# A sparse-attention layer on one core: the first stage's order of work, its input loads and its table stores are rewritten

## The chip, the cores and the metric

The kernel runs on one NeuronCore of one Trainium2 chip. The metric is device microseconds (us) of one execution. Five engines run at once, each through its own list of instructions in order: PE (TensorE: matmuls and transposes; its weight loads are listed as PEld), DVE (VectorE), ACT (ScalarE), POOL (GpSimd) and SP (SyncE, which here issues the DMAs). A tile scheduler orders each engine's list when the kernel is built and adds the semaphore waits.

## What is computed

One layer of native sparse attention with a gated branch, in float32, for 512 positions of width 1024, 16 heads of 64 in 4 groups:

```python
y = rms_norm(x, pre_gain)
q, kv, g, z = split_cols(y @ w_in, [1024, 6 * 256, 48, 3 * 1024])
k_c, v_c, k_s, v_s, k_w, v_w = split(kv, 6)
kc, vc = compress_kv(k_c, ...), compress_kv(v_c, ...)   # 31 blocks of 32 positions, + pos, then a 2-layer MLP
o_cmp, p_cmp = nsa_compressed(q, kc, vc, table)         # softmax(q kc + bias) vc
o_slc = nsa_selected(q, k_s, v_s, select_blocks(p_cmp), table)
o_win = nsa_window(q, k_w, v_w, table)
out = x + rms_norm((sum over 3 branches of gate * o * silu(z)) @ w_out, post_gain)
```

The bias of all three softmaxes comes from one table of 32 distance buckets by 16 heads.

## The kernel before

Every float32 product is made of three passes of a rounded type: each operand is split into a high part (a cast) and a low part (the operand less its high part), and PE adds high x high, low x high and high x low into one PSUM bank (`pass3`, L246). So each 512 KB weight tile `wr` (128x1024 numbers, 3 buffers) needs a cast into `wh` (L113 on ACT or L115 on DVE) and two subtractions into `wl` (L118, on POOL or DVE, 3 buffers each). Loads stand on SP's queue; a `wr` buffer is loaded again when its split is done, and `wh`, `wl` are written again when their matmuls are done. `tile_(n)` (L242) splits two tiles ahead; `order` (L226) lists the weights: 0, 1 for the compressed keys' projection `kc`, 2, 3 for `vc`, then four pairs (rows of the values' weights, rows of the keys' MLP weights `mk`), then pairs of key, query and gate weights with the values' MLP weights `mv`. Odd tiles are split on DVE alone, even ones on ACT and POOL (L240).

**The first stage** (L260 to L379) loads `x` in four tiles `xt` of 128 positions. `rms(t)` (L304) sums squares of a tile on ACT, and `rstd` (L84) makes the factor `r` on POOL in two steps. `prep(t)` (L311) does for each half of 512 columns: scale on DVE (L316), four transposes on PE into one bank (L321), two casts into `uh` (L327, ACT) and two subtractions into `ul` (L328, DVE). `uh`, `ul` are the normalized input, transposed, which every projection reads. `kc` is then made in two halves of 256 positions (`hh`, L368): per row block `k` and bank `m` the three passes in turn (L247 to L249, 96 matmuls of 256 columns). `prep(2)`, `prep(3)` stand inside the first half. `tables()` (L330) makes the bias table rows `toep` (4 matmuls, L344, L345) and the compressed branch's bias `cb` (16 matmuls of 16 columns, L351, L352), stores both to DRAM (L347, L356) and calls `load_bias(0)` (L160), which reads them back in shifted layouts.

**The second stage** (L381 on) makes `vc` (`half_t(2)`, `half_t(3)`: 48 matmuls of 512 columns into two `s` banks, L454), turns both projections into overlapping blocks (`blocks`: eight additions L407 from PSUM on DVE, then four casts and four subtractions L417 on DVE and POOL), and then runs the pairs: 24 matmuls of a value tile into four banks (`pj`, `pj`, `s`, `o`; L480 to L482) and 12 of an `mlp` (L425 to L427). After it come the keys, the queries, the gates, and from about 113 us the attention units, which the change doesn't touch.

Of the kernel before, what the change touches and what calls it, by code (L numbers as in the profile page):

```python
# [51 lines left out]
def nsa_layer(ctx: ExitStack, tc: tile.TileContext, x, pre_gain, post_gain, table, w_in, w_out,  # L52
# [39 lines left out]
    uh = [keep.tile([128, 2, S], F32R, name=f"uh{i}", tag="u", bufs=8) for i in range(4)]  # L92
    ul = [keep.tile([128, 2, S], F32R, name=f"ul{i}", tag="u", bufs=8) for i in range(4)]
# [152 lines left out]
    def pass3(po, wh_, wl_, rh, rl, first, last):  # L246
        T.matmul(po, wh_, rh, start=first, stop=False)  # L247
        T.matmul(po, wl_, rh, start=False, stop=False)  # L248
        T.matmul(po, wh_, rl, start=False, stop=last)  # L249

    def half_t(n, kh, banks):
        h, l = tile_(n)
        for kk in range(4):
            k = kh * 4 + kk
            for m, p in enumerate(banks):
                ms = slice(m * 128, m * 128 + 128)
                pass3(p, h[:, kk, ms], l[:, kk, ms], uh[k // 2][:, k % 2, :], ul[k // 2][:, k % 2, :],
                      k == 0, k == KT - 1)

    with tc.tile_pool(name="a1", bufs=1) as a1:  # L260
# [7 lines left out]
        V.tensor_copy(ones, one)  # L268
        xs = []
# [29 lines left out]
        banks = [tb, ob, tb]  # L299
        nb_ = 0  # L300

        rs_ = {}

        def rms(t):  # L304
            ss = a1.tile([128, 1], F32, name="ss", bufs=4)
            tc.keep_in_program_order(A.activation(sq, xs[t], AF.Square, scale=1.0 / 32, accum_out=ss))
            r = a1.tile([128, 1], F32, name="r", bufs=4)
            rstd(r, ss)
            rs_[t] = r

        def prep(t):  # L311
            nonlocal nb_
            r = rs_[t]
            for kq in range(2):
                hs = slice(kq * 512, (kq + 1) * 512)
                V.scalar_tensor_tensor(xs[t][:, hs], xs[t][:, hs], r, gain[kq], op0=ALU.mult, op1=ALU.mult)  # L316
                p = banks[nb_ % 3]()
                nb_ += 1
                for j in range(4):
                    k = kq * 4 + j  # L320
                    T.transpose(p[:, j * 128:(j + 1) * 128], xs[t][:, k * 128:(k + 1) * 128], ident)  # L321
                for jj in range(2):
                    i = kq * 2 + jj
                    src = p[:, jj * 256:(jj + 1) * 256].rearrange("p (a b) -> p a b", a=2)
                    dh = uh[i][:, :, t * 128:(t + 1) * 128]
                    dl = ul[i][:, :, t * 128:(t + 1) * 128]
                    A.copy(dh, src)  # L327
                    V.tensor_tensor(dl, src, dh.bitcast(F32), op=ALU.subtract)  # L328

        def tables():  # L330
            ntab = a1.tile([33, H], F32, name="ntab")
            V.tensor_scalar(ntab[0:32], tabx[0:32], -1.0, None, op0=ALU.mult)
            V.memset(ntab[32:33], BIG)
            nth = a1.tile([33, H], F32R, name="nth")
            ntl = a1.tile([33, H], F32R, name="ntl")
            V.tensor_copy(nth, ntab)
            V.tensor_tensor(ntl, ntab, nth.bitcast(F32), op=ALU.subtract)
            hsr = a1.tile([33, LT], F32R, name="hsr")
            hcr = a1.tile([33, D], F32R, name="hcr")
            A.copy(hsr, hots)  # L340
            A.copy(hcr, hotc)
# [19 lines left out]
        prep(0)  # L361
        split_ahead(0)
        prep(1)
        split_ahead(1)
        rms(2)
        rms(3)
        p_kc = [pj(), pj()]
        for hh in range(2):  # L368
            hs = slice(hh * 256, (hh + 1) * 256)
            for k in range(KT):  # L370
                if hh == 0 and k in (3, 5):
                    prep(2 if k == 3 else 3)
                h, l = tiles[k // 4]
                for m in range(2):
                    ms = slice(m * 128, m * 128 + 128)
                    pass3(p_kc[m][:, hs], h[:, k % 4, ms], l[:, k % 4, ms], uh[k // 2][:, k % 2, hs],
                          ul[k // 2][:, k % 2, hs], k == 0, k == KT - 1)
            if hh == 0:
                tables()  # L379

    with tc.tile_pool(name="a2", bufs=1) as a2:  # L381
        nb = G * NCMP

        def load_pos(nm):
            pr = small[nm, "p"]
            V.tensor_copy(pr[:, 1], pr[:, 0])
            p = tb()
            T.transpose(p[:, :32], pr.rearrange("p a b -> p (a b)"), ident[:32, :32])
            pt = sm.tile([128, 32], F32, name="pt" + nm)
            V.tensor_copy(pt, p[:, :32])  # L390
            return pt
# [10 lines left out]
        def blocks(banks, pt):  # L402
            blk = keep.tile([128, 16, G, NCMP], F32, name="blk", tag="kd", bufs=4)
            for m, p in enumerate(banks):
                for gp in range(2):
                    for lp in range(2):
                        V.tensor_tensor(  # L407
                            blk[lp * 64:lp * 64 + 64, :, 2 * m + gp, :],
                            view(p[gp * 64:gp * 64 + 64, :], lp, [[2, 16], [16, NCMP]]),
                            view(pt[gp * 64:gp * 64 + 64, :], lp, [[2, 16], [0, NCMP]]), op=ALU.add)  # L410
# [38 lines left out]

        kpt = load_pos("k")  # L450
        vpt = load_pos("v")
        kb = blocks(p_kc, kpt)
# [4 lines left out]
        kw2h, kw2l = load_w2("k", 2)  # L457
        vw2h, vw2l = load_w2("v", 1)
# [13 lines left out]
        for kp in range(4):  # L472
            h, l = tile_(n)
            for kk in range(2):
                k = kp * 2 + kk
                a, b = (v.rearrange("p (k a) c -> p k (a c)", k=2)[:, kk] for v in (h, l))
                for t in range(NT):
                    ts = slice(t * 128, (t + 1) * 128)
                    sh, sl = uh[k // 2][:, k % 2, ts], ul[k // 2][:, k % 2, ts]
# [4 lines left out]
            n += 2  # L484
        hs = silu2(p_mk)
# [307 lines left out]
    def split_y(g, qt):  # L793
        if g not in yhl:
# [3 lines left out]
            else:  # L798
                yhl[g] = [keep.tile([128, 2, S], F32R, name=f"y3{i}", tag="u", bufs=8) for i in range(2)]
# [20 lines left out]
    def wout():  # L820
        turn = [0, 3, 2, 1]
        og = [keep.tile([128, D], F32, name="og", tag="u", bufs=8) for _ in range(NT)]
# [38 lines left out]
        w3 = [wo_tile(3, 0, [keep.tile([128, 4, 256], F32R, name="w3", tag="u", bufs=8) for _ in range(2)]),  # L861
# [165 lines left out]
```

## Time and profile before

| | before |
|---|---|
| three timed runs | 466.29, 466.47, 467.47 us (median 466.47) |
| the profiled execution | 466.85 us, of which the span is 465.0 us |
| busy in the span | PE 450.9 us, PEld 375.3, DVE 330.6, ACT 274.3, POOL 184.7 |
| DMA | 44.63 MB, mean 96 GB/s |
| mean granted TensorE clock | 0.993 of full speed |

An engine's busy time says what it was doing, not what set the end. PE is busy nearly all the time, and its matmuls overlap (the end of each is modelled), so its pace is read from the distance between the starts of neighbours. Where PE loses time, a row shows either a gap and its releaser, or a longer distance between starts. The stretch from 0 to 45 us holds the work that the change rewrites.

### The profile page before, as it was taken

The page shows a single profiled execution, that of the slowest core. Times are in us where ns is not written, and L with a number is a line of the kernel's source. Part 1 is how long each engine was busy: PE and PEld are TensorE (multiplying, and loading weights), DVE is VectorE, ACT ScalarE, POOL GpSimd, SP SyncE. Part 2 cuts the span into 40 slices and gives each one's busy share as a digit, 9 for nine tenths or more (in the row PEclk, how much of TensorE's full clock was granted, in tenths as well). Part 3 has the DMA queues.
Part 4 walks back from the last instruction along what each step waited for, and adds up shares of the span by engine and source line. Part 5 has one row for each costly group of instructions (what it writes and reads, how often), then busy time and mean ns, then how long its engine had stood idle before and what let it go on. Part 6 is the DMA issues. An engine that isn't in the chain of part 4 may idle for free.

```text
span 465.0 us, 6924 instructions
## 1 busy us (share of the span) xinstructions
PE 450.9 (97%) x2330; PEld 375.3 (81%) x2330; DVE 330.6 (71%) x801; ACT 274.3 (59%) x642; POOL 184.7 (40%) x185
## 2 busy tenths in 40 slices
PE   5999999999999999999999999999999999999994
PEld 4797888878888878888888788888878888888883
DVE  6869844851766888768769776885896667567685
ACT  5712232542766577767846867666776666467541
POOL 4424544242223453342463525245343342448212
PEclk9989999999999999999999999999999999999998
DMA  8489275263111321511132332024051211214113
GB/s 300 142 82 280 77 216 162 66 206 90 47 45 48 112 59 34 182 45 47 45 90 70 88 94 71 21 57 132 19 180 45 92 45 47 91 43 140 47 45 135
DMA packets 45501, 44.63 MB, mean 96 GB/s; under 512 B 7751, under 2 KB 38471, under 8 KB 45466
## 3 DMA queue, kind: packets, MB, share of 16 engines
q1 hardware_dynamic: 44424, 44.00, 31.9%
q8 instruction: 18, 0.29, 0.3%
q10 hardware_dynamic: 1042, 0.20, 0.2%
q14 instruction: 17, 0.14, 0.1%
HBM read 41.99 MB, written 2.20 MB: 95 GB/s over the span
## 4 chain that ended last, share of the span: by engine, by line
PE 89%; DVE 4%; ACT 3%; issue 2%; POOL 1%; DVEq 0%; POOLq 0%; ACTq 0%
PE ps_pj L146 11%; PE ps_pj L148 11%; PE ps_pj L147 11%; PE ps_s L591 9%; PE ps_t L681 7%; PE ps_o L715 4%; PE ps_o L714 4%; PE ps_pj L834 3%; PE ps_pj L835 3%; PE ps_pj L836 3%; PE ps_s L247 2%; PE ps_s L248 2%; PE ps_s L249 2%; PE ps_pj L247 2%; PE ps_pj L248 1%
## 5 line engine op out<-in xcount | busy, mean ns | idle before, releaser
L118 POOL TENSOR_TENSOR wl<-wr,wh 128x512 fp32r<-128x512 f32 x94 | 123.0, 1328 | 138.6 <-ACT wh L113 122.2
L146 PE MATMUL ps_pj<-uh,wh 128*128 128x512 f32 x240 | 99.0, 412 | 0.0
L148 PE MATMUL ps_pj<-ul,wh 128*128 128x512 f32 x240 | 94.2, 393 | 0.0
L147 PE MATMUL ps_pj<-uh,wl 128*128 128x512 f32 x240 | 94.2, 392 | 0.0
L604 ACT ACTIVATE p<-p,nm 128x512 f32<-128x512 f32 (+3 forms) x128 | 71.6, 560 | 24.3 <-DVE nm L603 23.5
L685 DVE TENSOR_TENSOR ptl<-ps_t,pth 128x512 fp32r<-128x512 f32 x80 | 55.0, 688 | 28.2 <-ACT pth L684 27.7
L113 ACT CAST wh<-wr 128x1024 fp32r<-128x1024 f32 x47 | 49.2, 1047 | 43.5 <-DMA wr<-in_nsa_w_in_dram 20.1
L591 PE MATMUL ps_s<-kd,q 128*128 128x512 f32 (+5 forms) x256 | 63.9, 336 | 0.7 <-DVE zs L699 0.6
L684 ACT CAST pth<-ps_t 128x512 fp32r<-128x512 f32 x80 | 46.4, 580 | 29.3 <-PE ps_t L681 28.7
L148 PEld LDWEIGHTS ps_pj<-ul,wh 128*128 128x128 f32 x240 | 45.1, 188 | 10.1
L591 PEld LDWEIGHTS ps_s<-kd,q 128*128 128x128 f32 x256 | 43.9, 189 | 9.0 <-DVE zs L699 1.2
L146 PEld LDWEIGHTS ps_pj<-uh,wh 128*128 128x128 f32 x240 | 45.2, 188 | 6.1
L147 PEld LDWEIGHTS ps_pj<-uh,wl 128*128 128x128 f32 x240 | 45.3, 189 | 5.8
L603 DVE CUSTOM_DVE_ANT_0 p<-ps_s,bias 128x128 f32<-128x128 f32 (+3 forms) x80 | 34.6, 447 | 20.7 <-PE ps_s L591 20.5
L681 PE MATMUL ps_t<-ident,p 128*128 128x128 f32 x320 | 48.4, 272 | 0.0
L681 PEld LDWEIGHTS ps_t<-ident,p 128*128 128x128 f32 x320 | 39.7, 140 | 9.4
L714 PE MATMUL ps_o<-pth,vt 128*128 128x512 f32 x80 | 33.7, 421 | 0.0
L603 DVE CUSTOM_DVE_ANT_1 p<-ps_s,bias 128x256 f32<-128x256 f32 (+2 forms) x48 | 26.3, 555 | 9.3 <-PE ps_s L591 8.6
L728 POOL TENSOR_TENSOR y<-otmp,zs 128x256 f32<-128x256 f32 x16 | 12.3, 771 | 51.5 <-DVE otmp L725 51.5
L715 PE MATMUL ps_o<-ptl,vt 128*128 128x512 f32 x80 | 32.3, 404 | 0.0
L730 POOL TENSOR_TENSOR otmp<-otmp,zs 128x256 f32<-128x256 f32 x15 | 11.1, 741 | 37.9 <-DVE otmp L725 37.9
L569 ACT ACTIVATE zs<-ps_pj 128x512 f32<-128x512 f32 x22 | 13.1, 596 | 19.4 <-PE ps_pj L148 19.3
(268 smaller groups left out, 895.6 us busy)
## 6 DMA issues: line engine op xcount, KB each, us to landing
wr<-in_nsa_w_in_dram SPq DMA_DIRECT2D x36, 512.0 KB
wr<-in_nsa_w_in_dram SPq DMA_DIRECT2D x16, 256.0 KB
bias<-toepd SPq DMA_DIRECT2D x16, 256.0 KB
wr<-in_nsa_w_out_dram SPq DMA_DIRECT2D x8, 512.0 KB
xt<-in_x_dram SPq DMA_DIRECT2D x4, 512.0 KB
wr<-in_nsa_cmp_k_w_dram SPq DMA_DIRECT2D x4, 512.0 KB
wr<-in_nsa_cmp_v_w_dram SPq DMA_DIRECT2D x4, 512.0 KB
xr<-in_x_dram SPq DMA_DIRECT2D x8, 256.0 KB
```

Of the source, the lines that this page charges most:

```text
L113: A.copy(h[:, 0:kn], raw[:, 0:kn])
L118: el.tensor_tensor(l[:, ks], raw[:, ks], h[:, ks].bitcast(F32), op=ALU.subtract)
L146: T.matmul(p, a, rh, start=k == 0, stop=False)
L147: T.matmul(p, b, rh, start=False, stop=False)
L148: T.matmul(p, a, rl, start=False, stop=k == KT - 1)
L591: T.matmul(po, qs[h][:, qt * 128:(qt + 1) * 128], kds[h // R][:, i, c0:c0 + n], start=i == 0, stop=i == 1)
L603: V.tensor_tensor_reduce(pd, src, bi, 1.0, BIG, ALU.add, ALU.min, st["nm"][:, hh:hh + 1])
L604: A.activation(po, po, AF.Exp, bias=st["nm"][:, hh:hh + 1], scale=-1.0, accum_out=st["rs"][:, hh:hh + 1])
L681: T.transpose(tp[:, hh * 128:(hh + 1) * 128], st["p"][hh][:, c:c + 128], ident)
L685: V.tensor_tensor(pl, tp, ph.bitcast(F32), op=ALU.subtract)
L714: T.matmul(acc, v, ph, start=j == 0, stop=False)
L715: T.matmul(acc, v, pl, start=False, stop=j == qt)
```

## The change

`uh` and `ul` become two tiles of four row blocks each. The first two tiles of `x` are loaded in halves, and the squares of both are summed in halves too: tile 0's second half by one DVE instruction (L336 of the new kernel), the others on ACT. The weight loads 0, 1 and 2 stand between the loads of `x`. The first stage is written out by hand in fixed order (`put` keeps it): `sweep` (L381) does all high x high matmuls of a tile's half, then all with the low input, then all with the low weights, and yields between them. `kc`'s first 256 positions, `vc`'s first half for them (tile 2), then the same for the other 256 positions; `vc` now stands in two `o` banks, opened by a matmul of a zero row each (L379). Weights 1 and 3 are no longer cast on DVE: 1 is cast on ACT with its subtractions on DVE, 3 goes to ACT and POOL, and later odd tiles are cast on ACT with their subtractions on DVE. `load_pos`, `blocks` and the split of its result are separate functions. The tables' matmuls come after the sweeps; their stores (`cmpb` now in pieces of 128 B, 8 columns of 4 heads together, where they were 16 B) and `load_bias(0)` are issued later.

```diff
-            tiles.append(split_raw(raws[i], 4, *((V, V) if i % 2 else (A, P))))
+            tiles.append(split_raw(raws[i], 4, *((A, V) if i % 2 and i > 3 else (A, P))))
...
-            SP.dma_start(xt, x[t * 128:(t + 1) * 128, :])
+            for c in ((slice(0, 512), slice(512, D)) if t < 2 else (slice(0, D),)):
+                SP.dma_start(xt[:, c], x[t * 128:(t + 1) * 128, c])
             xs.append(xt)
-            if t == 1:
-                load_ahead(1)
+            if t:
+                load_ahead(t - 1)
...
+            for c, acc in ((0, ss), (512, s2)):
+                xc, junk = xs[t][:, c:c + 512], sq[:, c:c + 512]
+                if t == 0 and c:
+                    put(V.tensor_tensor_reduce(junk, xc, xc, 1.0 / D, 0.0, ALU.mult, ALU.add, acc))
+                else:
+                    put(A.activation(junk, xc, AF.Square, scale=1.0 / 32, accum_out=acc))
+            rstd(rs_[t], ss, s2)
...
+        def open_(ps_):
+            for p in ps_:
+                put(T.matmul(p, zrow, gh[:, 0:S], start=True, stop=False))
+
+        def sweep(n, ps_, kq, hs, opened=False):
+            h, l = tiles[n]
+            for w, u in ((h, uh), (h, ul), (l, uh)):
+                for kk in range(4):
+                    for m, p in enumerate(ps_):
+                        put(T.matmul(p[:, hs], w[:, kk, m * 128:(m + 1) * 128], u[kq][:, kk, hs],
+                                     start=not opened and kq == 0 and w is h and u is uh and kk == 0,
+                                     stop=kq == 1 and w is l and kk == 3))
+                yield
...
-            for g in range(G):
-                SP.dma_start(dview(cmpb, g * H * MC * R, [[R, 128], [128 * R, 8], [1, R]]), cb[:, g])
-            load_bias(0)
...
+        norm(1, 0, ob)
+        low(0, 0)
+        high(1, 0)
+        norm(1, 1, ob)
+        low(1, 0)
+        p_kc = [pj(), pj()]
+        run(sweep(0, p_kc, 0, h0))
...
+        run(sweep(0, p_kc, 0, h1))
+        with tc.issue_after(behind[0]):
+            kpt = load_pos("k")
+            vpt = load_pos("v")
+        run(sweep(1, p_kc, 1, h1))
+        kb = blocks(p_kc, kpt)
+        run(sweep(2, p_vc, 0, h1, True))
+        with tc.issue_after(behind[0]):
+            tables()
...
-        p_vc = [sb(), sb()]
-        half_t(2, 0, p_vc)
         half_t(3, 1, p_vc)
-        vb = blocks(p_vc, vpt)
+        SP.dma_start(toepd, toep)
+        for g in range(G):
+            SP.dma_start(dview(cmpb, g * H * MC * R, [[8 * R, 128], [1, 8 * R]]),
+                         small["cb"][:, g].rearrange("p j r -> p (j r)"))
+        vb = block_split(blocks(p_vc, vpt))
```

How the built lists differ, in three places. First PE's opening, from the first transposes on (`ident,xt` is a transpose; `uh_80`, `ul_84` are high and low input, new `uh_80`, `uh_81` the two halves of the rows and `ul_82`, `ul_83` their low parts). Before:

```order
L321 MATMUL ps_t<-ident,xt 128x128 x4
L321 MATMUL ps_o<-ident,xt 128x128 x4
L321 MATMUL ps_t<-ident,xt 128x128 x4
L247 MATMUL ps_pj<-uh_80,wh 128x256
L248 MATMUL ps_pj<-uh_80,wl 128x256
```

and now:

```order
L349 MATMUL ps_t<-ident,xt 128x128 x8
L349 MATMUL ps_o<-ident,xt 128x128 x8
L386 MATMUL ps_pj<-uh_80,wh 128x256 x8
L386 MATMUL ps_pj<-ul_82,wh 128x256 x8
L386 MATMUL ps_pj<-uh_80,wl 128x256 x8
L386 MATMUL ps_pj<-uh_81,wh 128x256 x8
```

Sixteen transposes stand ahead of the first projection matmul where twelve did, and the low weights' matmuls come last of each sweep.

Second, PE around the 16 narrow table matmuls (`nth,hcr`, `ntl,hcr`). Before, inside the second half of `kc`:

```order
L247 MATMUL ps_pj<-uh_80,wh 128x256
L248 MATMUL ps_pj<-uh_80,wl 128x256
L249 MATMUL ps_pj<-ul_84,wh 128x256
L351 MATMUL ps_s<-nth,hcr 128x16
L352 MATMUL ps_s<-ntl,hcr 128x16
```

and now, after ten of the 24 matmuls of `half_t(3)`:

```order
L248 MATMUL ps_o<-uh_81,wl 128x512
L249 MATMUL ps_o<-ul_83,wh 128x512
L247 MATMUL ps_o<-uh_81,wh 128x512
L412 MATMUL ps_s<-nth,hcr 128x16
L413 MATMUL ps_s<-ntl,hcr 128x16
```

All 16 still stand in one run; what is ahead of them and behind them are now matmuls of 512 columns.

Third, DVE where it makes the second compressed MLP's weights (`wl`) and evacuates the keys (`kd`). Before:

```order
L115 CAST wh<-wr 128x1024
L193 TENSOR_TENSOR kd<-ps_s,kd 64x512
L194 TENSOR_TENSOR kd<-ps_s,kd 64x512
L503 SCALAR_TENSOR_TENSOR kcl<-ps_t,kch 128x4x31
L193 TENSOR_TENSOR kd<-ps_s,kd 64x512
L194 TENSOR_TENSOR kd<-ps_s,kd 64x512
L193 TENSOR_TENSOR kd<-ps_s,kd 64x512
L194 TENSOR_TENSOR kd<-ps_s,kd 64x512
L118 TENSOR_TENSOR wl<-wr,wh 128x512
```

and now:

```order
L193 TENSOR_TENSOR kd<-ps_s,kd 64x512
L194 TENSOR_TENSOR kd<-ps_s,kd 64x512
L193 TENSOR_TENSOR kd<-ps_s,kd 64x512
L194 TENSOR_TENSOR kd<-ps_s,kd 64x512
L587 SCALAR_TENSOR_TENSOR kcl<-ps_t,kch 128x4x31
L118 TENSOR_TENSOR wl<-wr,wh 128x512
```

The cast is gone from DVE, and two of the six evacuations ahead of the subtraction now stand behind it. From the attention units on, every compute engine's list is the same as before.

## Rows read from the trace of the kernel before

**Rows 1.** The page: PE's busy time, and two groups of ACT (busy, mean ns | idle before).

```profile
PE 450.9 (97%) x2330; PEld 375.3 (81%) x2330; DVE 330.6 (71%) x801; ACT 274.3 (59%) x642; POOL 184.7 (40%) x185
...
L113 ACT CAST wh<-wr 128x1024 fp32r<-128x1024 f32 x47 | 49.2, 1047 | 43.5 <-DMA wr<-in_nsa_w_in_dram 20.1
...
L684 ACT CAST pth<-ps_t 128x512 fp32r<-128x512 f32 x80 | 46.4, 580 | 29.3 <-PE ps_t L681 28.7
```

**Rows 2.** What PE waited for, whole span (us in total, times, longest).

```profile
PE ps_s L480 <- DVE blk L407: 0.6, 1, 0.6
PE ps_t L321 <- issue: 0.6, 1, 0.6
...
PE ps_o L427 <- DVE wl L118: 0.4, 1, 0.4
```

**Rows 3.** Windows: us, busy PE, PEld, DVE, ACT, POOL, PEclk, DMA share, GB/s.

```profile
25.00:26.00 1.00, 1.00 (x6) 1.00 (x6) 0.72 (x4) 0.00 (x0) 0.35 (x1) 0.50 0.26 71
...
27.00:28.00 1.00, 1.00 (x6) 1.00 (x6) 0.39 (x1) 0.00 (x0) 0.00 (x0) 0.50 1.33 62
...
29.00:30.00 1.00, 1.00 (x11) 1.00 (x10) 1.00 (x3) 0.21 (x1) 0.00 (x0) 1.00 0.87 11
```

**Rows 4.** Timeline of PE (start us, duration us, engine, line).

```profile
10.24 0.58 PE L247 MATMUL ps_pj<-uh,wh 128*128 128x256 f32 x1 [0.46 <-ACT uh L327]
...
19.16 0.63 PE L321 MATMUL ps_t<-ident,xt 128*128 128x128 f32 x4 [0.57 <-issue]
19.72 0.41 PE L344 MATMUL ps_s<-hsr,nth 33*16 33x512 f32 x1
...
22.77 0.27 PE L351 MATMUL ps_s<-nth,hcr 33*128 33x16 f32 x1
...
24.64 0.58 PE L247 MATMUL ps_pj<-uh,wh 128*128 128x256 f32 x1
...
29.12 0.28 PE L247 MATMUL ps_pj<-uh,wh 128*128 128x256 f32 x1
29.24 0.28 PE L248 MATMUL ps_pj<-uh,wl 128*128 128x256 f32 x1
...
30.88 0.50 PE L247 MATMUL ps_s<-uh,wh 128*128 128x512 f32 x1
...
41.94 0.39 PE L480 MATMUL ps_pj<-wh,uh 128*128 128x512 f32 x1
```

**Rows 5.** Timeline of the opening: ACT, DVE and PE.

```profile
4.00 1.06 ACT L306 ACTIVATE sq<-xt 128x1024 f32<-128x1024 f32 x1 [1.23 <-DMA xt<-in_x_dram]
4.96 0.19 ACT L306 ACTIVATION_READ_ACCUMULATOR sq<-xt 128x1 f32 x1
...
5.42 1.06 ACT L306 ACTIVATE sq<-xt 128x1024 f32<-128x1024 f32 x1 [0.27 <-DMA xt<-in_x_dram]
...
6.15 2.18 DVE L316 SCALAR_TENSOR_TENSOR xt<-xt,r,ps_s 128x512 f32<-128x512 f32 x3 [1.96 <-POOL r L90]
...
6.96 1.12 PE L321 MATMUL ps_t<-ident,xt 128*128 128x128 f32 x4 [1.92 <-DVE xt L316]
```

**Rows 6.** Timeline of DVE and POOL: block additions, and low weights beside each other and alone.

```profile
31.15 5.49 DVE L407 TENSOR_TENSOR blk<-ps_pj,ptk 64x496 f32<-64x496 f32 x8
...
52.20 3.47 DVE L118 TENSOR_TENSOR wl<-wr,wh 128x512 fp32r<-128x512 f32 x2
...
56.38 1.29 DVE L118 TENSOR_TENSOR wl<-wr,wh 128x512 fp32r<-128x512 f32 x2
...
51.71 3.41 POOL L118 TENSOR_TENSOR wl<-wr,wh 128x512 fp32r<-128x512 f32 x2
```

**Rows 7.** Timeline of DVE and PE where the MLP's low weights come late.

```profile
88.16 1.53 DVE L118 TENSOR_TENSOR wl<-wr,wh 128x512 fp32r<-128x512 f32 x1
...
91.15 0.69 DVE L118 TENSOR_TENSOR wl<-wr,wh 128x512 fp32r<-128x512 f32 x1
...
91.89 0.38 PE L427 MATMUL ps_o<-wl,bh 128*124 128x256 f32 x1 [0.36 <-DVE wl L118]
```

More of the change, by code (lines that the diff above doesn't have):

```diff
@@ L256, in half_t, with load_pos, blocks @@
                 ms = slice(m * 128, m * 128 + 128)
-                pass3(p, h[:, kk, ms], l[:, kk, ms], uh[k // 2][:, k % 2, :], ul[k // 2][:, k % 2, :],
+                pass3(p, h[:, kk, ms], l[:, kk, ms], uh[k // 4][:, k % 4, :], ul[k // 4][:, k % 4, :],
                       k == 0, k == KT - 1)
+    def load_pos(nm):
+        pr = small[nm, "p"]
+        V.tensor_copy(pr[:, 1], pr[:, 0])
+        p = tb()
+        T.transpose(p[:, :32], pr.rearrange("p a b -> p (a b)"), ident[:32, :32])
+        pt = sm.tile([128, 32], F32, name="pt" + nm)
+        V.tensor_copy(pt, p[:, :32])
+        return pt
+    def blocks(banks, pt):
+        blk = keep.tile([128, 16, G, NCMP], F32, name="blk", tag="kd", bufs=4)
+        for m, p in enumerate(banks):
+            for gp in range(2):
+                for lp in range(2):
+                    V.tensor_tensor(
+                        blk[lp * 64:lp * 64 + 64, :, 2 * m + gp, :],
+                        view(p[gp * 64:gp * 64 + 64, :], lp, [[2, 16], [16, NCMP]]),
+                        view(pt[gp * 64:gp * 64 + 64, :], lp, [[2, 16], [0, NCMP]]), op=ALU.add)
+        return blk
     with tc.tile_pool(name="a1", bufs=1) as a1:
@@ L298, in nsa_layer @@
         sq = a1.tile([128, D], F32, name="sq")
-        banks = [tb, ob, tb]
-        nb_ = 0
-        rs_ = {}
+        put = tc.keep_in_program_order
+        rs_, pt_, behind = {}, {}, []
         def rms(t):
             ss = a1.tile([128, 1], F32, name="ss", bufs=4)
[L306 to L328, printed above, removed]
@@ new lines, in part, with high, low, split_first @@
+        def part(u, t, kq):
+            return u[kq][:, :, t * 128:(t + 1) * 128], pt_[t, kq].rearrange("p (a b) -> p a b", a=4)
+        def high(t, kq):
+            put(A.copy(*part(uh, t, kq)))
+        def low(t, kq):
+            d, p = part(ul, t, kq)
+            i = put(V.tensor_tensor(d, p, part(uh, t, kq)[0].bitcast(F32), op=ALU.subtract))
+            behind[:] = [i.ins]
+        def split_first(n, el=P):
+            h = wp.tile([128, 4, 256], F32R, name="wh", tag="wh", bufs=3)
+            l = wp.tile([128, 4, 256], F32R, name="wl", tag="wl", bufs=3)
+            put(A.copy(h, raws[n]))
+            tiles.append((h, l))
+            def rest(i):
+                ks = slice(i * 2, i * 2 + 2)
+                put(el.tensor_tensor(l[:, ks], raws[n][:, ks], h[:, ks].bitcast(F32), op=ALU.subtract))
+            return rest
@@ L365, in nsa_layer @@
+        high(0, 0)
+        norm(0, 1, tb)
+        w0 = split_first(0)
+        w0(0)
+        w0(1)
+        norm(1, 0, ob)
[5 more added lines that the diff above has]
+        run(sweep(0, p_kc, 0, h0))
+        high(0, 1)
+        high(1, 1)
+        low(0, 1)
+        low(1, 1)
         rms(2)
+        w1 = split_first(1, V)
+        w1(0)
+        w1(1)
         rms(3)
[L367 to L379, printed above, removed]
+        w2 = split_first(2)
@@ new lines, in nsa_layer @@
+        w2(0)
+        w2(1)
+        s1 = sweep(1, p_kc, 1, h0)
+        next(s1)
+        next(s1)
+        norm(2, 0, tb)
+        high(2, 0)
+        run(s1)
+        norm(2, 1, tb)
+        high(2, 1)
+        scale(3, 0)
+        low(2, 0)
+        low(2, 1)
+        p_vc = [ob(), ob()]
+        open_(p_vc)
+        s2 = sweep(2, p_vc, 0, h0, True)
+        next(s2)
+        turn_(3, 0, tb)
+        high(3, 0)
+        scale(3, 1)
+        next(s2)
+        turn_(3, 1, tb)
+        high(3, 1)
@@ L381, in nsa_layer @@
+        low(3, 0)
+        low(3, 1)
+        run(s2)
+        run(sweep(0, p_kc, 0, h1))
[7 more added lines that the diff above has]
+            tables()
     with tc.tile_pool(name="a2", bufs=1) as a2:
         nb = G * NCMP
[L384 to L391, printed above, removed]
@@ L400, in load_w2, with block_split @@
             return h.rearrange("p k d c -> p k (d c)"), l.rearrange("p k d c -> p k (d c)")
[L402 to L410, printed above, removed]
+        def block_split(blk):
             bh = a2.tile([128, 16, nb], F32R, name="bh", tag="bh", bufs=2)
```

66 lines of the change are left out of this document (43 added, 23 removed).

## The prediction

> **What bounds the kernel now.** I read the page's busy times first: PE is busy for 450.9 us of a span of 465.0 [rows 1], so a change of order alone can give back only what PE loses. Then the list of what PE waited for [rows 2]: no entry names a DMA, and the three rows shown sum to 1.6 us. Gaps are therefore a small part, and the rest has to be read from PE's pace, in windows and in the distance between starts. At full clock a 256-column matmul takes 0.12 us (29.12 to 29.24 in [rows 4]); 48 of 512 columns take 11.06 us (30.88 to 41.94), 0.23 each. [...]
>
> So the change can act in one stretch: from the first projection matmul at 10.24 us to the first matmul of the value rows at 41.94 us [rows 4], 31.70 us. Its work at full clock: 96 matmuls of `kc` at 0.12, 11.5 us; 48 of `vc`, 11.1; 16 narrow ones, 1.9 (22.77 to 24.64); five groups of four transposes at 0.56 (19.16 to 19.72), 2.8; four wider table matmuls and two small transposes, 1.0 at most, an estimate from the neighbours' starts at 0.2 to 0.25 each. That is 28.3 us, and **3.4 us are lost**. The low clock cost 1.5 of these: 24.64 to 28.0 held 16 matmuls, worth 1.9 us at 0.12, in 3.4. The other 1.9 are waits for late input tiles (the row at 19.16 has one of 0.57) and the slow first matmuls.
>
> **The change, part by part.**
>
> *The opening.* The first squares start at 4.00 on a whole tile, the next tile is there by 5.42 [rows 5]: 1.42 us per 512 KB, 0.71 per half. Halves land at about 3.3, 4.0, 4.7 and 5.4. DVE squares tile 0's second half from 4.0; the trace has no such instruction on SBUF alone, so between 0.65 (a subtraction alone, [rows 6]) and 0.73 (a scaling, 2.18 for three, [rows 5]): done by 4.75, where ACT's sum was done at 5.15 (4.96 and 0.19). With POOL's two steps, 1.0 us from there to 6.15, the first scaling starts near 5.7, 0.45 earlier. This is not passed on: four more transposes now stand ahead of the first sweep, and DVE's list has the first low input between the third and the fourth scaling. Walked through: transposes of the first block 6.5 to 7.6 (1.12, [rows 5]); its cast 0.58 [rows 1], 8.2; its low part at 0.69, 8.9 (0.69 is one block addition, 5.49 over eight, [rows 6]); the fourth scaling 0.73, 9.65; its four transposes 0.5 to 1.1. The first sweep starts between 10.1 and 10.7; I take 10.3, against 10.24. **Gain 0**, though four transposes (0.56) now lie ahead of the stretch.
>
> *The sweeps.* Same matmuls, other order. `vc`'s tile 2 goes from 24 of 512 columns to 48 of 256: 48 x 0.12 less 24 x 0.23 is +0.24. The two opening matmuls add 2 x 0.23 = 0.46. With the transposes, -0.56, the work grows by **0.1**. What waits remain: the second sweep needs tile 1's cast on ACT, behind the four casts of the first two input tiles (0.58 each), one sum of squares (1.15) and a cast of 1.05 [rows 1]: it ends near 13.4, when the first sweep's 24 x 0.12 end. The transposes of tile 2 need a scaling that now stands behind tile 1's two subtractions on DVE, ready near 15.6 where PE comes at 15.4. I allow 0.2 for that and 0.4 for the slow start: **0.6** in place of 1.9. Bounds: 0, and the old 1.9, if in-order lists merely exchange one late input for another.
>
> *The table matmuls.* Not removed; they stand in one run of 16 within `half_t(3)`. Their own 1.9 us stays. Whether the clock falls behind them again decides 1.5 us. In favour of a fall: the run is as long and as narrow as before, and PE was busy when it fell. Against: 512-column matmuls now surround it, where table matmuls, transposes and a 0.57 us gap stood in the 5 us before it. Bounds 0 and 1.5; I take **1.5 again**, since the row nearest to it is that same run. [...]
>
> *Banks and DVE.* `vc` moves from the `s` to the `o` banks, so the value rows' matmuls wait for the first four of eight block additions (4 x 0.69) in another bank: PE's list has ten matmuls, 2.3 us, ahead of it, as before. The 0.6 us wait of [rows 2] stays, if DVE is free when `vc` ends. DVE has about 10 to 13 us of work in the 11 us before that: eight additions 5.5, the table's copies about 1.2, two subtractions of weights and two of blocks, each 0.65 alone and 1.73 while POOL subtracts too (3.47 against 1.29 for two, [rows 6]). Cost **0**, bounded by 0 and about 2.
>
> *Later odd tiles.* Their cast goes from DVE to ACT (1.05 us, [rows 1]), hidden by ACT's slack. The one place where PE waited for such a tile is at 91.89 [rows 7]: the low weights were made on DVE at 88.16 (1.53, beside POOL) and 91.15, behind the keys' evacuations. Now the cast is off DVE and the first subtraction stands two evacuations earlier: by the row durations done near 87 and 91, half a us ahead of need. **Gain 0.36**; the low bound is 0.
>
> *Stores, bias loads, input order.* No PE wait names a DMA [rows 2], so moving them behind weights gains 0. They delay nothing either: after the move by the splits that its loads queue behind, the bias of the first unit is in SBUF near 50 us (an estimate), and the units begin at about 113. Weight tiles 8 to 11 queue behind the stores on SP, but each cast also waits for its buffers, which come free later. If that cover failed, one load's 1.4 us (the 512 KB above) would show.
>
> Sum: -(1.9 - 0.6) + 0.1 - 0.36 = **-1.6 us** with the low clock again. The profiled execution took 466.85, 0.38 above the median of the three runs, 466.47. On its own time the sum gives 465.25; on the median, 464.9. I give the median's.
>
> **The rivals.**
>
> 1. *The clock holds* behind the narrow run, for the reasons above: 1.5 us more, 463.4.
> 2. *The change does not do what it says*: PE exchanges waits for others in the in-order lists of DVE and ACT (DVE's second weight subtraction waits for a cast on ACT with three scalings behind it), the low clock returns, and only the 0.36 is kept: 1.9 lost again and 0.1 added, 466.2. For it: DVE and ACT feed PE alternately from 6 to 20 us. Against: sweeps leave 24 matmuls, 2.9 us, between needs.
> 3. *Slower: DVE comes late to `vc`.* Its subtractions collide with POOL's (1.73 for 0.65) and wait, through reused memory, for the narrow matmuls, so the block additions start late and the value rows' `o` bank with them. PE's wait is the delay plus 2.75 (four additions) less 2.3 (ten matmuls): delay + 0.45, in place of 0.6. Starting from -1.6, the time is over 0.3% higher only from a delay of 3.2 us; at 3.4 it would be 468.1. Before, the additions began at once behind the last sum. The collisions alone give (1.73 - 0.65) x 4 = 4.3 us of more DVE work, of which about 2 are covered.
>
> **How the numbers follow.** 0.3% is 1.4 us, about what a measurement of this kernel can tell from no change: below 465.07 is faster, above 467.87 slower. The chances: the forecast 0.45 (464.3 to 466.2 by its waits of 0 to 1.9), rival one 0.34 (462.8 to 464.7 likewise), rival two 0.14, rival three 0.07. Faster: all of rival one and over half of the forecast, 0.27, together 0.61. Slower: 0.07. The same: the rest, 0.32. The range reaches from 462.9 to 466.4: it leaves out rival three, the tail of rival two and the best of rival one, not over 2 in 10.
>
> **What would show it.** Right: the first sweep at about 10.3 us; the value rows' first matmul near 40.7 (39.2 if the clock holds); a granted clock of 0.50 behind the narrow matmuls; a wait of about 0.6 for an `o` bank; no wait for low weights near 90 us. Wrong: a PE wait for a weight load, a first sweep after 11 us, sweeps with gaps of over 1 us, or block additions for `vc` starting more than 1 us behind its last matmul.

## The result and the profile after

The changed kernel takes **470.87 us** (median of 11 runs, 468.21 to 472.17) beside 466.47 us for the kernel before on the same chip: ratio **1.0078, 95% interval [1.0058, 1.0098]**. It is slower, by 0.8%; 464.9 was forecast. The profiled execution took 471.52 us, its span 469.7.

The page's busy times come first (compare [rows 1]): PE is busy 3.9 us longer than before, DVE 9.3 us less.

```profile
PE 454.8 (97%) x2356; PEld 379.2 (81%) x2356; DVE 321.3 (68%) x783; ACT 283.6 (60%) x647; POOL 186.2 (40%) x187
```

What PE waited for, over the whole span (us in total, times, longest). The waits of the opening have grown: 2.6 for tile 0's transposes, before 1.9 [rows 5], and 1.5 for tile 1's, before 0.4 (the last row here). The 0.6 us wait for a bank of the block additions [rows 2] is gone.

```profile
PE ps_t L349 <- DVE xt L343: 2.6, 1, 2.6
PE ps_o L349 <- DVE xt L343: 1.5, 1, 1.5
...
PE ps_t L521 <- DVE hs L515: 0.5, 1, 0.5
PE ps_o L509 <- DVE wl L118: 0.3, 1, 0.3
```

```profile
PE ps_o L321 <- DVE xt L316: 0.4, 1, 0.4
```

ACT's squares in the opening (start us, duration). Tile 0's first half is read at 3.38 as forecast, tile 1's at 5.56 and 8.43; whole tiles were read at 4.00 and 5.42 [rows 5].

```profile
3.38 0.63 ACT L338 ACTIVATE sq<-xt 128x512 f32<-128x512 f32 x1 [0.60 <-DMA xt<-in_x_dram]
...
5.56 0.63 ACT L338 ACTIVATE sq<-xt 128x512 f32<-128x512 f32 x1 [1.46 <-DMA xt<-in_x_dram]
...
8.43 0.63 ACT L338 ACTIVATE sq<-xt 128x512 f32<-128x512 f32 x1 [2.14 <-DMA xt<-in_x_dram]
```

PE's timeline. The first sweep matmul starts at 13.06 where the first projection matmul of before started at 10.24 [rows 4]; the 16 narrow matmuls take from 37.80 to 41.70, 3.9 us, where they took 1.9; the value rows' first matmul (L563) comes at 46.59, before at 41.94.

```profile
13.06 2.06 PE L386 MATMUL ps_pj<-uh,wh 128*128 128x256 f32 x8
14.91 1.26 PE L386 MATMUL ps_pj<-ul,wh 128*128 128x256 f32 x8
16.01 1.12 PE L386 MATMUL ps_pj<-uh,wl 128*128 128x256 f32 x8
...
37.80 0.40 PE L412 MATMUL ps_s<-nth,hcr 33*128 33x16 f32 x1
...
41.39 0.38 PE L413 MATMUL ps_s<-ntl,hcr 33*128 33x16 f32 x1
41.70 0.50 PE L248 MATMUL ps_o<-uh,wl 128*128 128x512 f32 x1
...
46.59 0.40 PE L563 MATMUL ps_pj<-wh,uh 128*128 128x512 f32 x1
```

Their weight loads take 0.33 us instead of 0.19: first the changed kernel's PEld, then that of before.

```profile
38.25 0.33 PEld L412 LDWEIGHTS ps_s<-nth,hcr 33*128 33x128 f32 x1
```

```profile
22.87 0.19 PEld L352 LDWEIGHTS ps_s<-ntl,hcr 33*128 33x128 f32 x1
```

Behind the narrow matmuls the granted clock is 0.50 again, as in the windows at 25 and 27 us of [rows 3]; columns as there.

```profile
42.00:43.00 1.00, 1.00 (x5) 0.79 (x4) 0.61 (x2) 1.00 (x3) 0.40 (x1) 0.78 0.00 0
43.00:44.00 1.00, 1.00 (x4) 0.81 (x3) 0.67 (x2) 0.98 (x2) 0.96 (x1) 0.50 0.74 126
```

So the value rows start 4.65 us later than before: 2.8 from the opening and 2.0 from the narrow matmuls, less 0.2 from the rest of the stretch. The clock's dip is in both kernels. From there on the two profiles stay level (spans 469.7 and 465.0). Against the forecast of 40.7 the value rows are 5.9 late: 2.8 in the opening, 2.0 in the narrow matmuls, and over half of the rest in the first sweep, whose first 16 matmuls took 2.95 us (13.06 to 16.01) where 1.9 and 0.4 for the slow start were allowed.

### The profile page after: what moved, and what is told of

The parts are those of the page before. It is cut to its first block, busy times and chain, and to the rows that moved or that the text cites. A ratio compares the mean times of both kernels' runs of the same rounds, so it can differ in the third digit from the quotient of the medians.

```text
span 469.7 us, 6981 instructions
## 1 busy us (share of the span) xinstructions
PE 454.8 (97%) x2356; PEld 379.2 (81%) x2356; DVE 321.3 (68%) x783; ACT 283.6 (60%) x647; POOL 186.2 (40%) x187
## 4 chain that ended last, share of the span: by engine, by line
PE 85%; DVE 7%; ACT 3%; DMA 2%; issue 1%; POOL 0%; SPq 0%; DVEq 0%; POOLq 0%; ACTq 0%
PE ps_pj L146 11%; PE ps_pj L148 11%; PE ps_pj L147 11%; PE ps_s L675 8%; PE ps_t L765 7%; PE ps_o L799 4%; PE ps_o L798 4%; PE ps_pj L919 3%; PE ps_pj L920 3%; PE ps_pj L921 3%; PE ps_pj L386 3%; PE ps_s L782 1%; DMA xt<-in_x_dram 1%; PE ps_s L249 1%; PE ps_s L248 1%
## 5 line engine op out<-in xcount | busy, mean ns | idle before, releaser
L118 POOL TENSOR_TENSOR wl<-wr,wh 128x512 fp32r<-128x512 f32 x92 | 120.2, 1325 | 138.4 <-ACT wh L113 114.2
L113 ACT CAST wh<-wr 128x1024 fp32r<-128x1024 f32 x55 | 57.5, 1047 | 44.5 <-PE ps_s L249 13.5
L118 DVE TENSOR_TENSOR wl<-wr,wh 128x512 fp32r<-128x512 f32 x18 | 16.6, 958 | 13.6 <-ACT wh L113 13.4
```

The lines of the kernel that those rows point to most:

```text
L113: A.copy(h[:, 0:kn], raw[:, 0:kn])
L118: el.tensor_tensor(l[:, ks], raw[:, ks], h[:, ks].bitcast(F32), op=ALU.subtract)
```

## The experiments

In each run the kernel before ran on the same chip, and the ratio is to it. Edits that do not name another kernel are to the changed one.

### Undoing one part, or doing one alone

**Whole input tiles** (e1_whole_x).

```diff
-for c in ((slice(0, 512), slice(512, D)) if t < 2 else (slice(0, D),)):
+for c in (slice(0, D),):
```

> The changed kernel with the first two input tiles loaded whole again; their squares are still taken in halves, everything else is as changed. Theory (the halved loads, whose rows are 2 KB instead of 4 KB, land later: the second half of tile 1 was first read at 8.43 us where whole tiles were read at 4.00 and 5.42): the square of tile 1 starts by about 5.5 us, the first sweep matmul comes at 10.3 to 10.8 us instead of 13.06, the whole opening moves up by 2.3 to 2.8 us and the time with it, 470.9 to about 468.3 us (ratio to the kernel before 1.003 to 1.005). Rival (the weight tile's load, issued right behind tile 1, or the order of the loads delays x, not the halving): tile 1 is still read after 8 us and the time stays at 470.5 to 471.

Measured 468.84 us, ratio 1.0040 [1.0027, 1.0054], 1.8 us less than the changed kernel by the ratios. Tile 1 is read at 5.46 and the first sweep starts at 10.74:

```profile
5.46 0.63 ACT L338 ACTIVATE sq<-xt 128x512 f32<-128x512 f32 x1 [0.71 <-DMA xt<-in_x_dram]
```

```profile
10.74 0.56 PE L386 MATMUL ps_pj<-uh,wh 128*128 128x256 f32 x1
```

The halved loads cost the opening 2.3 us in this profile; the order of the loads did not.

**Contiguous weights** (e2_contiguous_weights), the 128 B pieces kept.

```diff
-put(A.copy(hcr, hotc))
+put(A.copy(hcr.rearrange("p (j m) -> p m j", j=8), hotc.rearrange("p (m j) -> p m j", j=8)))
-hcj = hcr.rearrange("p (m j) -> p j m", j=8)
+hcj = hcr.rearrange("p (j m) -> p j m", j=8)
```

> The changed kernel with one edit: the ScalarE cast of the 0/1 table writes its columns in the permuted order, so that the sixteen narrow matmuls load weights that lie side by side instead of with a step of 8 elements; the 128 B store pieces stay. Theory (the step makes each weight load 0.33 us instead of 0.19, and the narrow matmuls wait for it): the narrow matmuls' pace goes from 0.238 to about 0.114 us, their stretch from 3.9 to 1.9 us, and the time from 470.9 to about 469.0 us (ratio 1.003 to 1.005). Rival (the narrow matmuls are slow from their place in the program or from the clock there): pace 0.23 again and no change of the time (470.5 to 471).

Measured 467.41 us, ratio 0.9998 [0.9980, 1.0016]: 3.7 us less by the ratios, twice the forecast. The weight loads are back at 0.19 and the stretch at 1.9 us, and in the profiled execution the clock does not fall behind it, which is the other half of the gain in that profile. Over the executions that half stays open: the six with a mean clock of 0.996 or more and the six below it both average 467.3.

```profile
37.41 0.19 PEld L413 LDWEIGHTS ps_s<-ntl,hcr 33*128 33x128 f32 x1
```

```profile
41.00:42.00 1.00, 1.00 (x6) 0.84 (x5) 1.00 (x1) 0.46 (x1) 1.00 (x2) 1.00 1.23 256
```

**The kernel before with halved tiles** (e3_before_halved_x: its `SP.dma_start(xt, ...)` for tiles 0 and 1 in the two column halves).

> The kernel before with one edit: the first two input tiles are loaded in two halves of 512 columns each. Theory (halving by columns makes x land later by itself): the first square starts a little earlier or at the same 4.0 us (it needs both halves here), the square of tile 1 1 to 3 us later than 5.42 us, the first sweep matmul 1 to 3 us after 10.24, and the time is 467.5 to 469.5 us (ratio 1.002 to 1.006). Rival (the halves are harmless without the new order of loads): square of tile 1 by 5.6 us and 466.2 to 466.8 us.

Measured 468.51 us, 1.0033 [1.0018, 1.0048]. Tile 1 is read at 6.79, the first projection matmul comes at 11.32. Halving is a loss in the old order too, 1.5 us by the ratio.

```profile
6.79 1.06 ACT L307 ACTIVATE sq<-xt 128x1024 f32<-128x1024 f32 x1 [1.33 <-DMA xt<-in_x_dram]
```

**The kernel before with 128 B pieces** (e4_before_128B: its two narrow matmuls take `hcj[:, j]` with the step of 8, and its stores have the new pattern).

> The kernel before with one edit: the table's rows are written in 128 B pieces, for which the narrow matmuls take their weights with a step of 8 elements, as in the changed kernel; place and order of the stores stay as before. Theory (the stepped weights cost 1.9 us on TensorE, the pieces give nothing on the path): narrow matmuls at a pace of 0.23 us, their stretch 1.9 to 3.9 us long, and the time 467.5 to 468.6 us (ratio 1.002 to 1.005). Rival (stores four times shorter free the queue for the bias and weights behind them, and something on the path ends earlier; or the pace stays at 0.114): 465 to 466.5 us.

Measured 469.33 us, 1.0050 [1.0035, 1.0065]; the narrow stretch takes 3.9 us at a pace of 0.238, and the clock falls behind it, to 0.53 from 30 to 32 us.

### Both losses undone

c1_whole_x_contiguous has both edits.

> The changed kernel with both edits that helped by themselves: input tiles 0 and 1 loaded whole, and the 0/1 table cast into the permuted order so that the narrow matmuls load contiguous weights. Theory (the two losses are separate terms on TensorE's path and add): ratio to the kernel before 1.0040 + 0.9998 - 1.0078 = 0.996, about 465.6 us; first sweep matmul at 10.5 to 10.8 us, narrow matmuls at a pace of 0.114 us, value rows' first matmul at 40.5 to 41 us if the clock holds, some 42 if not. Rival (the two losses cover one another, a wait further on takes one of them): ratio 0.999 to 1.001, a wait of 1.5 us or more between 40 and 110 us that the changed kernel doesn't have.

Measured 465.75 us, **0.9968 [0.9954, 0.9982]**; on another chip (d1_both_again, the same kernel) 465.49 us, **0.9975 [0.9963, 0.9986]**. The losses add, and what is left of the change beats the kernel before, by 0.25 to 0.32%.

> The kernel with both edits (whole tiles, contiguous weights), unchanged, on the chip of the three kernels beside it. Theory (what it gains on the kernel before does not hang on the chip or on a lucky clock): ratio to before 0.995 to 0.998. Rival (its gain was a clock that happened to hold): 0.998 to 1.001, with mean granted clocks of 0.992 to 0.996 in most executions.

Its PE timeline: first sweep 10.59, value rows 39.64, granted clock 1.00 between.

```profile
10.59 1.19 PE L386 MATMUL ps_pj<-uh,wh 128*128 128x256 f32 x8
11.62 1.12 PE L386 MATMUL ps_pj<-ul,wh 128*128 128x256 f32 x8
12.58 1.12 PE L386 MATMUL ps_pj<-uh,wl 128*128 128x256 f32 x8
...
36.91 0.39 PE L247 MATMUL ps_o<-uh,wh 128*128 128x512 f32 x1
...
37.60 0.39 PE L247 MATMUL ps_o<-uh,wh 128*128 128x512 f32 x1
...
39.64 0.39 PE L563 MATMUL ps_pj<-wh,uh 128*128 128x512 f32 x1
```

The edits below are to this kernel ("both edits").

### The clock

**Narrow matmuls twice** (c2_narrow_twice: `for j in [*range(8)] * 2:`).

> The kernel with both edits (whole tiles, contiguous weights) and the sixteen narrow matmuls issued twice, the second set writing the same values over the first: 32 narrow matmuls at the fast pace, a stretch about as long (3.7 us) as that of the sixteen slow ones. Theory (TensorE's clock is lowered behind a long stretch of narrow matmuls, whatever makes it long): granted clock 0.50 for some 3 us behind it, as in the changed kernel, so 1.85 us of work and 1.5 us of clock more than without the second set: about 469 us if that is 465.6. Rival (the slow weight loads are what lowers it): granted clock 1.00 behind it, 1.85 us more, about 467.4 us.

Measured 469.24 us, 1.0048 [1.0027, 1.0070], 3.7 us above both edits by the ratios, as the first theory has it. The weight loads are fast here (0.19 us), and the clock falls all the same:

```profile
42.00:43.00 1.00, 1.00 (x4) 0.81 (x3) 0.17 (x1) 0.00 (x0) 1.00 (x1) 0.50 0.41 58
```

**Narrow matmuls spread** (d5_narrow_spread): two behind each group of three wide ones.

```diff
-half_t(3, 1, p_vc)
+for kk in range(4):
+    for m, p in enumerate(p_vc):
+        ...
+        narrow(kk * 2 + m)
```

> The kernel with both edits and the sixteen narrow matmuls set two by two behind each group of three wide ones of the compressed values' last half tile, in place of one stretch. Theory (without a stretch of narrow matmuls TensorE's clock stays up in every execution): granted clock 1.00 from 30 to 48 us, mean clock 0.998 or more in all executions, 0 to 0.8 us faster than the kernel with both edits on the same chip. Rival (the clock falls elsewhere or for another reason): clocks below 0.996 in some executions, same time or slower.

Measured 467.19 us, 1.0018 [1.0007, 1.0029]. The mean clock is 0.996 to 0.999 in all 12 executions, so the dip is avoided, but the time is 2.0 us higher by the ratios: a miss. The mean clock of the kernel with both edits is as high on this chip (0.996 to 0.999, d1), so there was nothing to win, and PE's timeline shows what was lost.

```profile
36.06 0.25 PE L413 MATMUL ps_s<-ntl,hcr 33*128 33x16 f32 x1
36.24 0.51 PE L486 MATMUL ps_o<-uh,wh 128*128 128x512 f32 x1
36.59 0.40 PE L487 MATMUL ps_o<-uh,wl 128*128 128x512 f32 x1
36.82 0.40 PE L488 MATMUL ps_o<-ul,wh 128*128 128x512 f32 x1
37.15 0.27 PE L412 MATMUL ps_s<-nth,hcr 33*128 33x16 f32 x1
...
37.46 0.50 PE L486 MATMUL ps_o<-uh,wh 128*128 128x512 f32 x1
```

A group of three and two takes 1.22 us (36.24 to 37.46). Three wide ones alone take 0.69 (36.91 to 37.60 above), two narrow ones 0.22. Going from wide matmuls to narrow ones and back thus costs 0.3 us, eight times 2.4; whether the 33 operand rows, the 16 columns or the change of bank does it isn't shown.

### What makes halved tiles late

**Halves from two queues** (c3_halves_two_queues: contiguous weights, halved tiles, `(A if t == 1 else SP).dma_start(...)`).

> The changed kernel with contiguous weights for the narrow matmuls and the input halved as it is there, but the two halves of tile 1 issued from ScalarE's queue, beside those of tile 0 on SP's. Theory A (the halves land late because SP issues them one behind another, 0.45 us each, and the transfers behind them crowd in): tile 1's second half is read by 5.5 to 6.5 us, first sweep matmul at 11 to 11.5 us, about 1.5 us less than with one queue (467.4): 466. Theory B (the 2 KB rows themselves move slower at the start: 225 to 262 GB/s between 3 and 6 us against 350 to 381): tile 1's second half is still read at 7 us or later, first sweep after 12 us, 467 to 468.

Measured 469.26 us, 1.0049 [1.0030, 1.0068]. All four halves are issued by 2.2 us; ACT reads tile 1's at 5.99 and 8.62. Theory A is out. Theory B has the place of tile 1 right but not the time, which is 2.4 us above the same kernel with one queue (e2) by the ratios.

**Halves by rows** (c5_halved_by_rows, two loads of 64 rows of 4 KB per tile).

> The kernel with both edits, but tiles 0 and 1 each loaded in two loads of 64 rows of 4 KB: as many loads as with the halves by columns, with whole rows. Theory (the 2 KB rows make the halves land late): lands as with whole tiles, tile 1's square by 5.6 us, first sweep matmul at about 11 us, 465.5 to 466.2 us. Rival (the number of loads in flight does it): tile 1's second half at 7 us or later, first sweep at 12 to 13 us, 467 to 468.

Measured 470.27 us, 1.0060 [1.0038, 1.0081]: tile 0 is read at 5.32, tile 1 at 8.12. My theory of short rows isn't needed then: with rows as long as before, two loads per tile are as late. One rival is left, that loads of 64 partitions are slow for a reason of their own. Bytes moved per us show the lag, first for this kernel, then for the changed one, last for the kernel before, where both tiles were in by 5.42.

```profile
4.00:5.00 1.00, 1.00 (x2) 0.28 (x1) 0.26 (x1) 0.00 (x0) 0.00 (x0) 1.00 1.06 188
5.00:6.00 1.00, 0.10 (x1) 0.00 (x0) 0.62 (x2) 0.68 (x2) 0.00 (x0) 1.00 1.04 266
```

```profile
4.00:5.00 1.00, 1.00 (x2) 0.28 (x1) 0.28 (x2) 0.10 (x2) 0.00 (x0) 1.00 0.84 236
5.00:6.00 1.00, 0.00 (x1) 0.00 (x0) 0.58 (x2) 0.44 (x1) 0.23 (x1) 1.00 0.69 225
```

```profile
4.00:5.00 1.00, 1.00 (x2) 0.28 (x1) 0.19 (x1) 1.00 (x2) 0.00 (x0) 1.00 0.95 370
```

The 470.27 us are above both forecasts; this profile also has the low clock behind its narrow matmuls (0.50 from 41 to 44 us).

**Tile 0 alone halved** (c8_first_tile_halved).

> The kernel with both edits, with tile 0 alone loaded in column halves and tile 1 whole. Theory (each load of 2 KB rows slows the transfers beside it): tile 0's first half is squared at 3.4 us, its second not before 4.7, tile 1 lands at 6 to 7 us, first sweep 0.5 to 1.2 us later than 11.05, 466.2 to 467 us. Rival (only the halves of tile 1, which are last among them, are late): first sweep at 11 us or sooner, 465 to 465.8.

Measured 468.31 us, 1.0043 [1.0024, 1.0062]. Tile 1, whole, is read at 6.23, later than without the halves; the first sweep comes at 11.24, only 0.2 us behind the 11.05 of c1. The profile has the low clock behind the narrow matmuls too (0.50 from 38 to 41 us), which c1's doesn't. The executions spread from 466.44 to 470.55, and the profiled one (467.14) is among the quick; where the others lost more isn't shown. Even one tile in two loads brings no gain.

### The other parts

**Old split of the odd weight tiles** (c4_old_odd_tiles: `(V, V)` in place of `(A, V)`).

> The kernel with both edits (whole tiles, contiguous weights) and, beside that, the odd weight tiles from the fifth on split on VectorE alone again, as in the kernel before, instead of cast by ScalarE and subtracted by VectorE. Theory (the ScalarE casts stand ahead of the tanh of the compression and cost TensorE about 0.46 us near 107 us, which the changed split was forecast to gain near 91 us): 0.3 to 0.6 us faster than with the new split, about 465.1 us if that is 465.6. Rival (VectorE, without that help, is late with weights near 91 us as before, and gives the gain back): the same within 0.3 us.

Measured 467.58 us, 1.0006 [0.9989, 1.0023]: 1.8 us slower than with the new split, the opposite of the theory, and not at 91 us. DVE's additions for `vc` start at 42.16 instead of 40.35 (a weight subtraction of 1.77 us now stands ahead), and PE waits for the bank:

```profile
38.82 1.77 DVE L118 TENSOR_TENSOR wl<-wr,wh 128x512 fp32r<-128x512 f32 x1
40.51 1.72 DVE L499 TENSOR_TENSOR bl<-blk,bh 128x496 fp32r<-128x496 f32 x1
42.16 5.48 DVE L274 TENSOR_TENSOR blk<-ps_o,ptv 64x496 f32<-64x496 f32 x8
```

```profile
45.02 0.47 PE L563 MATMUL ps_o<-wh,uh 128*128 128x512 f32 x1 [1.94 <-DVE blk L274]
```

In this profile the granted clock is up behind the narrow matmuls and falls behind that wait instead, to 0.50 from 47 to 49 us.

**The new split alone in the kernel before** (d3_before_odd_tiles).

> The kernel before with the new split of the odd weight tiles from the sixth on alone (cast by ScalarE, subtracted by VectorE). Theory (the relief of VectorE is worth something only where the sweeps have brought the value rows forward, so that their bank waits for VectorE): 0 to 0.4 us faster than before, the 0.6 us wait for the bank near 44.5 us shorter. Rival (the relief alone carries the gain of 1.5 us that is left once both losses are undone): 1 to 2 us faster.

Measured 468.83 us, 1.0055 [1.0039, 1.0072]: slower by 2.6 us, a miss for both. One part is the edit's: PE waits 1.0 us where it didn't, since ACT's casts stand ahead of the MLP's tanh. Most of the rest of the profiled one lies in the opening, where the first weight tile landed later (its cast at 8.67, before 7.17), which the edit doesn't touch; how often that happens is open.

```profile
PE ps_t L439 <- DVE hs L433: 1.0, 1, 1.0
```

**16 B pieces** (c6_16B_pieces: the old store pattern at the new place, plain cast).

> The kernel with both edits, but the table's rows stored in 16 B pieces as in the kernel before (at the new place, behind the value rows' weights). Theory (the stores' length is off every path): the same within 0.3 us, 465.7. Rival (the short pieces hold the queues while the bias and weights pass them, which was what the 128 B pieces are for): 0.5 to 2 us slower, with a wait for a weight tile or a bias behind 42 us.

Measured 467.02 us, 1.0002 [0.9988, 1.0016], and again beside both edits on one chip (d2_16B_again) 466.55 us, 1.0000 [0.9984, 1.0015], against 465.49:

> The kernel with both edits and the stores in 16 B pieces, beside the one with 128 B pieces on one chip. Theory (the pieces cost nothing, the 1.0002 measured apart from it came of the clock): within 0.3 us of the kernel beside it. Rival (the short pieces cost time by themselves): 0.8 to 1.8 us slower than it.

The short pieces cost about 1.1 us on that chip. SP's list of d2 shows how (issue start, duration): the bias loads behind the stores are slow to issue, the first two 3.44 us where d1 has 0.98, and the weight tiles that went out at 51.36 with 128 B pieces go at 55.26. First d1's row, then d2's.

```profile
51.36 0.90 SPq L103 DMA_DIRECT2D wr<-in_nsa_w_in_dram  x2
```

```profile
47.00 3.44 SPq L163 DMA_DIRECT2D bias<-toepd  x2
50.48 2.55 SPq L168 DMA_DIRECT2D cbs<-cmpb  x4
53.08 1.77 SPq L163 DMA_DIRECT2D bias<-toepd  x2
55.26 0.38 SPq L103 DMA_DIRECT2D wr<-in_nsa_w_in_dram  x1
```

PE then waits for a weight tile's high and low parts, 0.98 us in all:

```profile
61.61 0.50 PE L562 MATMUL ps_pj<-wh,uh 128*128 128x512 f32 x1 [0.30 <-ACT wh L113]
...
63.02 0.50 PE L564 MATMUL ps_pj<-wl,uh 128*128 128x512 f32 x1 [0.68 <-POOL wl L118]
```

The profile of c6 has neither wait: the clock fell behind its narrow matmuls, and PE came to these matmuls 1.3 us later than in d1. Its narrow matmuls have contiguous weights and take 1.9 us:

```profile
38.00:39.00 1.00, 1.00 (x4) 0.81 (x3) 0.67 (x2) 0.84 (x2) 1.00 (x1) 0.50 1.11 300
```

**First sweep sooner** (c7_sweep_sooner: its first eight matmuls ahead of tile 1's last transposes).

> The kernel with both edits and the first eight sweep matmuls issued ahead of the transposes of tile 1's second half, which they don't need. Theory (TensorE waits 0.35 us for these transposes' input while the first sweep's operands are nearly there): first sweep matmul at 10.5 to 10.7 us instead of 11.05, 0.3 to 0.6 us faster, about 465.3. Rival (the later transposes and the casts behind them make the next sweep wait for as long): no change, 465.5 to 466.

Measured 468.85 us, 1.0034 [1.0018, 1.0050], a miss: the sweep starts at 10.56 but runs at half pace for longer (2.08 and 1.70 us for eight, above 1.19 and 1.12), and its third group comes at 14.68 instead of 12.58.

```profile
10.56 2.08 PE L386 MATMUL ps_pj<-uh,wh 128*128 128x256 f32 x8 [0.68 <-ACT uh L359]
...
13.14 1.70 PE L386 MATMUL ps_pj<-ul,wh 128*128 128x256 f32 x8
14.68 1.12 PE L386 MATMUL ps_pj<-uh,wl 128*128 128x256 f32 x8
```

## Why the prediction was wrong

- **The opening ("Gain 0") failed.** Its step "Halves land at about 3.3, 4.0, 4.7 and 5.4" divided one rate of 512 KB loads by two. They were read at 3.38, 4.88, 5.56 and 8.43, and the first sweep came 2.8 us after 10.24. Runs e1, e3 and c5 put this on two loads per tile, by columns or by rows; what in the DMA does it stays open. Tile 0's first half was read sooner, at 3.38 against 4.00; tile 1's last later, at 8.43 against 5.42, and the DMA engines weren't idle (0.84 and 0.69 busy in the windows above).
- **The table matmuls ("Their own 1.9 us stays") failed.** I priced the moved matmuls by rows of the old ones and overlooked that `hcj` gives them weights with a step of 8 elements. Loading 128 columns then takes 0.33 us instead of 0.19, PE's pace follows (0.24 us from start to start, before 0.11), and 16 take 3.9 us. e2 and e4 agree: with contiguous weights a load takes 0.19 us and the 16 matmuls 1.9 (e2), with the step they take 3.9 in the old kernel too (e4). What in the step makes the load slow isn't shown.
- **The clock ("1.5 again") came out, but the run was not the one that I priced.** The fall that the 1.5 prices is the 0.50 of [rows 3], with PE busy 1.00. The 14 wide matmuls behind the narrow ones took 4.89 us (41.70 to 46.59), in d1 3.29, so the dip cost 1.6 (before it was 1.6 as well: 15 matmuls and not 16 stand in 24.64 to 28.01). I had taken the run to be "as long and as narrow as before"; it was twice as long. With 3.7 to 3.9 us of narrow matmuls the clock falls in every profile (to 0.50 in c2 and the changed kernel, 0.53 in e4), with fast loads (c2) or slow (the changed kernel, e1, e4). With 1.9 us of them between the same wide matmuls it holds behind them in seven profiles (e2, c1, d1, c3, c4, c7, d2) and falls in three (c5, c6, c8). So without the step of 8 rival 1 was open; what decides between the two stays open. The term was no constant before either. In all 18 profiles a mean granted clock of 0.996 or more goes with no fall before 50 us, and one of 0.995 or less with a fall. Of 29 executions of the kernel before on d1's chip, 17 have a mean granted clock up to 0.994 and average 467.3 us, 12 have 0.996 or more and average 466.1.
- **The sweeps fell short in the changed kernel.** From first sweep to value rows I had 28.3 + 0.1 + 0.6 = 29.0 us without the clock's dip. The changed kernel has 33.53 (13.06 to 46.59), less 2.0 for the narrow matmuls and 1.6 for the dip 29.9. Before it was 31.70, less its own dip 30.1, so the gain is 0.2 where 1.2 was forecast. The term that was mis-sized most is the slow start: 0.4 allowed, 1.0 measured in the first 16 matmuls. The slow start varies from execution to execution. In d1, where it took 0.1, the stretch is 39.64 - 10.59 = 29.05, in c1, the same kernel, 29.54. That d1 meets the sum is in part luck: it has none of the waits that I allowed for, and four groups of transposes took 1.6 us where I priced 2.2, but its 144 sweep matmuls took 18.0 where 144 x 0.12 is 17.3. No wait interrupts the sweeps of the changed kernel: PE is busy throughout from 15 to 34.4 us.
- **Banks and DVE ("Cost 0"): no cost came, but by a part priced elsewhere.** The `o` bank's wait, forecast at 0.6 as before, is 0 in the changed kernel and 0.22 in d1. Without the new split of the odd tiles it is 1.94 (c4): rival 3's mechanism, which that split averts. I had written only its later gain.
- **Later odd tiles (-0.36) failed.** The wait for low weights is still 0.3 (L509), and a new one of 0.5 (L521) follows, since ACT's casts stand ahead of the tanh; c4, without these casts on ACT, doesn't have it.
- **Stores (0) was mis-sized.** At the new place 128 B pieces are worth about 1.1 us (c6, d2). "They delay nothing either" holds for these pieces alone. As written, with stepped weights, the kernel pays 2.0 us and the clock's dip for them.

With both losses undone the profiled spans differ by 2.0 us (465.0 before, with the dip, and 463.0 in d1, without it). My terms with the clock held (rival 1) give 3.1. Of the 1.1 that lack, 0.4 lies ahead of the value rows (39.64, where 39.2 was forecast) and the rest behind them: 0.36 not gained and a new wait. So most of the 2.0 is the clock. All 12 executions of d1 have a mean clock of 0.996 or more and average 465.5 us, 0.6 less than the 12 like them of the kernel before; the rest of the 1.2 to 1.5 us that the ratios show is that the clock holds more often.

The forecast's sign was lost to two prices taken over from rows of another shape.

## What to carry to other kernels

When a store is reshaped, follow the new index back to the matmul's stationary operand: give the step to an engine with slack (here a ScalarE cast that writes permuted) and keep weights contiguous (0.19 us a load here, 0.33 with the step). Before an input load is cut in two to start sooner, while more loads are issued right behind it, compare when the *last* piece lands: here it landed later each time that both tiles were cut (read at 6.79 to 8.62 us, uncut at 5.33 to 5.87). A price read from a row holds for that row's shape and access pattern only. The fastest version here keeps the change with both of these corrected: 0.9968 and 0.9975 of the time before, about half of it from a clock that falls less often.

## What was not expected of the hardware

- Two loads per 512 KB tile landed later than one, with whole rows too: tile 1's last part was read at 6.79 to 8.62 us (e3 to c3), whole tiles at 5.33 to 5.87 (d3 to c4).
- Alternating narrow matmuls of 33 operand rows and wide ones of 128 cost 0.3 us per pair of changes (d5).
- The granted clock fell, to 0.50, with PE busy 1.00 throughout, behind the same 1.9 us of narrow matmuls in some profiles and not in others; behind 3.7 to 3.9 us of them it fell in every one.
- The first eight 256-column matmuls took 1.85 us instead of 0.96 (13.06 to 14.91), while the profile shows a granted clock of 1.00; in the two profiles of the kernel with both edits they took 1.03 and 1.61.
